# RWKV units of a hybrid diffusion step: half-height chunk factors, chain products in one tile shape, triangular inversion from 16-blocks through DRAM

## Chip, cores, metric

The kernel runs on one core of a Trainium2 chip. The metric is the device time of one execution in microseconds (us); the figure quoted is the median of the runs of one kernel. Engines: PE (TensorE products; PEld is its weight load), DVE (VectorE), ACT (ScalarE), POOL (GpSimd), SP (SyncE, which here only issues DMAs).

## What is computed

Two groups of tokens, 512 latent ones and 128 context ones, pass two layers of SwiGLU, token mixing and SwiGLU. The change lies in the mixing of layer 0, whose RWKV-7 half is, per head and direction, a scan over the tokens:

```python
def step(S, inp):
    r_t, w_t, k_t, v_t, kk_t, a_t = inp
    sa = jnp.einsum('bhvk,bhk->bhv', S, -kk_t)
    S = (S * w_t[:, :, None, :] + sa[..., None] * (kk_t * a_t)[:, :, None, :]
         + v_t[..., None] * k_t[:, :, None, :])
    return S, jnp.einsum('bhvk,bhk->bhv', S, r_t)
...
for d, (wd, ad) in enumerate(((wd_f, ad_f), (wd_b, ad_b))):
    ...
    yd, sd = wkv_scan(r32, decay, kd, v32, kk, a, s0[:, d], reverse=(d == 1))
```

There are 8 heads of 64 and two directions. The other half of the mixing is attention (8 query heads, 128 queries at a time); both end in one output projection. All of it is float32.

## The kernel before

The order of instructions on the engines' queues comes from a scheduler that works on a simulated timeline; the program's own order ranks what is ready. Loads are kept in order behind one another (`load`, L73).

Layer 0's mixing has a stage of its own, `rwkv_attention` (from L669), that runs from about 728 to 1366 us of the trace. Its work is cut into 4 units of two heads, each unit in both directions and in 10 chunks of 64 tokens. Each unit has four parts, all generators, and `take` lets them take turns:

- `rwkv_prep` loads r, k and v of the unit (one buffer each for r and k, so the loads for the next unit wait for this one's last reader), makes the decays, the scaled factors and, per chunk, one 128 x 256 product `pA` (L1020). Its stationary side `bk` holds b and k of both heads on 128 partitions; its moving side `arb` holds a and r of each head with zeros in the other head's rows. So L1000 to L1003 work on 64 partitions at a time, and L1004 copies the half that counts into `ar`. The product, masked (L1024), is `am`. The transposes of `bk` are `bt` (L1030, L1032).
- `tri_inverse` turns the strictly triangular 64 x 64 part of each of the unit's 40 chunk matrices (10 chunks, 2 directions, 2 heads) into the inverse of I - A. DVE block transposes bring the two 32 x 32 diagonal blocks to one chunk per partition (L1180), 30 steps of a multiply and an add on growing and shrinking blocks solve them (L1189, L1191), more transposes bring them back (L1199, L1202), and two rounds of 40 products of 32 x 32 make the block off the diagonal (L1210, L1218).
- `rwkv_chain` has 10 jobs, 8 latent and 2 context chunks, each for two heads and two directions. One after the other: `am` by values and `ar` by state into PSUM (L1086, L1097), a copy to `rt` (L1099), the inverse times `rt` (L1102), a copy to `uv` (L1104), the next state from the identity times the old state plus `bt` times `uv` (L1090, L1110), scaled by the decay (L1113), and the read-out in PSUM `ps_yr` from `uv` and from the state (L1121, L1123), added to `yb` (L1128).
- `rwkv_out` normalises, gates and stores `yc` (L1158).

Attention (`att_block`, 40 blocks) is put between them by `take`; its results go out by SP (L893). The context's final states go out by SP too (L1138), and their tile shares its one buffer with the next unit's initial states. PSUM tiles of tag `ps` have 3 buffers while the stage runs, `pn` 2 and `pb` 1; a tag's buffers are given out in program order. The order of the parts is:

```python
take(28, 5, prep(0))
take(16, 4, inv(0), prep(1))
take(12, 8, chain(0), inv(1))
take(10, 7, chain(1), prep(2), out(0))
take(12, 9, out(1), inv(2), prep(3))
take(12, 5, inv(3), chain(2))
take(12, 2, out(2), chain(3))
take(4, 0, out(3))
```

A product in float32 shows in the trace as two pairs of a weight load and a matmul; "x8" is four products.

Of the kernel before, what the change touches and what calls it, by code (L numbers as in the profile page):

```python
# [9 lines left out]
F32 = mybir.dt.float32  # L10
# [21 lines left out]
class K:  # L32
    """The network on one core. Activations are feature-major: [features, tokens]."""
# [29 lines left out]
    def open_res(self):  # L63
        """temporaries, weights raw and in two parts, input of the next product, residual."""
# [6 lines left out]
    def load(self, dst, src):  # L71
        """a load that the scheduler keeps behind the load before it."""
# [28 lines left out]
    def setup(self):  # L101
        """parameters and tokens; the loads that the first sub-layer waits for come first."""
# [11 lines left out]
            # these wait until the first sub-layer runs  # L114
# [7 lines left out]
        def rows_of(name):  # L122
            """rows of parameters ..."""
# [11 lines left out]
        def columns(name, rows):  # L135
            """... turned into one scalar per partition."""
# [26 lines left out]
        # silu of both condition vectors; 32 stationary columns, of which 2 are in use  # L163
# [15 lines left out]
        # tokens, feature-major  # L179
# [18 lines left out]
                # 1 + the bias of scale; gain of the output times the weight of the residual  # L198
# [40 lines left out]
    def ada(self, l, j, parts):  # L239
        """pieces of work that make mods[l, j][:, part, d, group]: shift, scale, gate of sub-layer j of layer l."""  # L240
# [13 lines left out]
    def ada_piece(self, l, j, part, t, w=None):  # L254
        """two of the eight input tiles; four groups of 256 outputs go to as many column groups of the array."""
# [24 lines left out]
        if part:  # L280
            # gain * (1 + scale), or weight * gate * gain
# [383 lines left out]
    def rwkv_attention(self):  # L665
# [5 lines left out]
        for h in range(2):  # L671
            self.nc.gpsimd.memset(self.arb[64 - 64 * h:128 - 64 * h, :, h], 0.0)
# [496 lines left out]
    def tri_inverse(self, u):  # L1169
# [15 lines left out]
        for s in range(1, 31):  # L1185
# [6 lines left out]
            if s % 6 == 0:  # L1192
                yield
# [705 lines left out]
```

## Time and profile before

| what | us |
|---|---|
| median of 3 runs (3339.91 to 3350.36) | 3347.76 |
| span of the profiled execution, first to last instruction | 3337.1 |
| PE busy in it | 3091.3 |
| DVE busy | 1923.3 |
| ACT busy | 1210.2 |
| POOL busy | 683.2 |

The profiled execution has no time of its own beside its span; the median of the runs stands 10.7 us above it, which is 0.3%. The chain of work that ended last is 80% PE and 10% DVE. Over most of the span PE is 90% busy or more; the slices from 728 to 1366 us, the stage of the change, are where it is not, and where the granted TensorE clock is lowest. Inside that stage the engines take turns at being the bound, so it is read in seven parts, by the parts of `take`.

### The profile page before, as it was taken

What the parts mean: (1) busy time and instruction counts of PE and PEld (TensorE: products, weight loads), DVE (VectorE), ACT (ScalarE), POOL (GpSimd) and SP (SyncE); (2) the same over time, 40 slices, a digit from 0 to 9 for tenths busy, and PEclk for the clock granted to TensorE, in tenths of its full rate; (3) what the DMA queues carried; (4) which work ended last, traced back from release to release, by engine and by line L of the source; (5) the groups of instructions that cost most, each with busy time, mean ns of one, the idle gap of its engine ahead of it and who ended that gap; (6) DMA issues with size and microseconds to landing.
All of it is one profiled execution on the core that took longest, in us unless ns stands there. A gap on an engine that the chain in (4) does not pass through costs nothing.

```text
span 3337.1 us, 55197 instructions
## 1 busy us (share of the span) xinstructions
PE 3091.3 (93%) x22259; PEld 2857.2 (86%) x22259; DVE 1923.3 (58%) x3731; ACT 1210.2 (36%) x2491; POOL 683.2 (20%) x795
## 2 busy tenths in 40 slices
PE   7999999986789789899999999999997689999998
PEld 6999998974576567789999999999996579999998
DVE  5433357428735861475466686666487955733346
ACT  4422235325334432453332453233353235422223
POOL 1000014132001200153333231233142533100002
PEclk8999999987778796899999999999998789999998
DMA  6433245620000000735443445454358863342223
GB/s 223 153 101 127 99 136 183 220 84 17 5 21 15 13 7 3 199 109 159 142 153 122 155 137 167 138 165 142 115 139 204 272 204 120 108 139 76 76 89 108
DMA packets 333924, 404.44 MB, mean 121 GB/s; under 512 B 42217, under 2 KB 299174, under 8 KB 333414
## 3 DMA queue, kind: packets, MB, share of 16 engines
q1 hardware_dynamic: 319174, 361.96, 34.4%
q0 software_dynamic: 14496, 38.97, 3.9%
q8 instruction: 175, 2.87, 0.4%
q14 instruction: 79, 0.65, 0.1%
HBM read 356.79 MB, written 42.89 MB: 120 GB/s over the span
## 4 chain that ended last, share of the span: by engine, by line
PE 80%; DVE 10%; issue 3%; POOL 2%; DMA 2%; ACT 2%; SPq 0%; POOLq 0%; DVEq 0%; ACTq 0%
PE ps_h L428 9%; PE ps_h L429 9%; PE ps_h L430 9%; PE ps_wide L428 5%; PE ps_wide L429 5%; PE ps_wide L430 5%; PE ps_y L428 5%; PE ps_y L430 5%; PE ps_y L429 5%; PE ps_wide L263 2%; PE ps_yr L1123 1%; PE ps_A L1020 1%; PE ps_pt L929 1%; PE ps_yr L1121 1%; DVE s5x L1564 1%
## 5 line engine op out<-in xcount | busy, mean ns | idle before, releaser
L401 DVE TENSOR_TENSOR wlo<-w,whi 128x1024 fp32r<-128x1024 f32 (+2 forms) x574 | 572.6, 1005 | 384.2 <-ACT whi L400 374.4
L400 ACT CAST whi<-w 128x1024 fp32r<-128x1024 f32 (+2 forms) x576 | 483.0, 847 | 857.0 <-PE ps_h L429 288.0
L428 PE MATMUL ps_h<-hh,whi 128*128 128x320 f32 x2112 | 658.0, 312 | 3.7 <-ACT hh L345 2.4
L429 PE MATMUL ps_h<-hl,whi 128*128 128x320 f32 x2112 | 656.7, 311 | 0.3 <-DVE hl L346 0.3
L430 PE MATMUL ps_h<-hh,wlo 128*128 128x320 f32 x2112 | 656.3, 311 | 0.0
L428 PEld LDWEIGHTS ps_h<-hh,whi 128*128 128x128 f32 x2112 | 399.2, 189 | 9.9 <-issue 3.4
L429 PEld LDWEIGHTS ps_h<-hl,whi 128*128 128x128 f32 x2112 | 398.8, 189 | 2.6 <-issue 1.5
L430 PEld LDWEIGHTS ps_h<-hh,wlo 128*128 128x128 f32 x2112 | 398.8, 189 | 1.1 <-issue 0.8
L429 PE MATMUL ps_y<-gl,whi 128*128 128x320 f32 x1056 | 325.8, 310 | 0.0
L430 PE MATMUL ps_y<-gh,wlo 128*128 128x320 f32 x1056 | 325.3, 310 | 0.0
L428 PE MATMUL ps_y<-gh,whi 128*128 128x320 f32 x1056 | 323.8, 311 | 1.1 <-ACT y L519 1.0
L428 PE MATMUL ps_wide<-hh,whi 128*128 128x320 f32 x912 | 288.6, 316 | 10.6 <-ACT y L653 4.4
L429 PE MATMUL ps_wide<-hl,whi 128*128 128x320 f32 x912 | 286.4, 314 | 1.3 <-DVE hl L346 1.2
L430 PE MATMUL ps_wide<-hh,wlo 128*128 128x320 f32 x912 | 285.3, 313 | 0.0
L362 POOL TENSOR_TENSOR ssy<-ssy,sq 128x320 f32<-128x320 f32 x84 | 96.0, 1142 | 566.1 <-ACT sq L361 563.5
L428 PEld LDWEIGHTS ps_y<-gh,whi 128*128 128x128 f32 x1056 | 197.1, 188 | 6.5 <-ACT y L519 2.2
L430 PEld LDWEIGHTS ps_y<-gh,wlo 128*128 128x128 f32 x1056 | 197.9, 188 | 1.0 <-issue 0.8
L429 PEld LDWEIGHTS ps_y<-gl,whi 128*128 128x128 f32 x1056 | 198.2, 188 | 0.7 <-issue 0.5
L428 PEld LDWEIGHTS ps_wide<-hh,whi 128*128 128x128 f32 x912 | 174.2, 191 | 17.9 <-issue 5.3
L470 DVE SCALAR_TENSOR_TENSOR g<-th,ps_h 128x320 f32<-128x320 f32 x159 | 77.0, 485 | 175.9 <-PE ps_h L430 175.3
L429 PEld LDWEIGHTS ps_wide<-hl,whi 128*128 128x128 f32 x912 | 173.7, 190 | 3.3 <-DVE hl L346 1.9
L430 PEld LDWEIGHTS ps_wide<-hh,wlo 128*128 128x128 f32 x912 | 173.6, 190 | 0.6 <-DVE wlo L401 0.3
(461 smaller groups left out, 5916.8 us busy)
## 6 DMA issues: line engine op xcount, KB each, us to landing
w<-in_ffn_w_dram SPq DMA_DIRECT2D x120, 1024.0 KB
ada_w<-in_ada_w_dram SPq DMA_DIRECT2D x72, 1024.0 KB
w<-in_ffn_w_dram SPq DMA_DIRECT2D x112, 512.0 KB
w<-in_ab_w_in_dram SPq DMA_DIRECT2D x14, 1024.0 KB
s5cd<-s_work POOLq DMA_DIRECT2D x128, 64.0 KB, 2.4
s5bd<-s_st POOLq DMA_DIRECT2D x32, 256.0 KB, 3.1
s5bt<-s5bd SPq DMA_DIRECT2D x32, 256.0 KB
w<-in_s_w_out_dram SPq DMA_DIRECT2D x8, 1024.0 KB
```

The costliest lines, as they stand in the source:

```text
L263: nc.tensor.matmul(ps[32 * g:32 * g + 32, :256], self.sc[:, 2 * t + k, :], w[:, k, g * 256:g * 256 + 256], start=(t + k == 0), stop=(2 * t ...
L362: nc.gpsimd.tensor_tensor(ss, ss, sq, op=OP.add)
L400: a = self.nc.scalar.copy(hi[:, :kt], s)
L401: v = (eng or self.nc.vector).tensor_tensor(lo[:, :kt], s, hi[:, :kt].bitcast(F32), op=OP.subtract)
L428: nc.tensor.matmul(o, hi[:, k], ah[k][half], start=(k == 0), stop=False)
L429: nc.tensor.matmul(o, hi[:, k], al[k][half], start=False, stop=False)
L430: self.last[0] = nc.tensor.matmul(o, lo[:, k], ah[k][half], start=False, stop=(k == kt - 1))
L470: nc.vector.scalar_tensor_tensor(g, t, 0.5, p3[:, :HALF], op0=OP.mult, op1=OP.mult)
L929: nc.tensor.matmul(po, self.vt[:, b, rows], pts[:, n], start=(n == 0), stop=(n == nkt - 1))
L1020: nc.tensor.matmul(pA[:, j % 2 * 256:j % 2 * 256 + 256], bk[:, j].rearrange("p a t -> p (a t)"), arb[:, j].rearrange("p h a t -> p (h a t) ...
L1121: nc.tensor.matmul(py[hr, col(d)], uv[:, d, p, h], rv(am[:, d, p, h, 64:]), start=True, stop=first)
L1123: nc.tensor.matmul(py[hr, col(d)], s[hr, d, p], rv(u["ar"][d][hr, self.chunk(d, p), 1]), start=False, stop=True)
```

## The change

It touches the four units alone (and removes comments elsewhere). The diff, cut to its core:

```diff
 rwkv_attention:
-        self.arb = self.mixe.tile([128, 10, 2, 2, 64], F32, name="arb")
+        self.st = [self.mixb.tile([128, 2, 2, 64], F32, name=f"st{k}") for k in range(4)]
+        for t in self.st:
+            for h in range(2):
+                mset(t[64 - 64 * h:128 - 64 * h, :, h], 0.0)
+        self.dx = [self.mixe.tile([128, 20, 64], F32, name=f"inv_d{k}") for k in range(2)]
+        self.invd = [self.dram.tile([2, 80, 256], F32, name=f"invd{k}") for k in range(2)]
+        self.invx = [self.dram.tile([2, 2, 80, 256], F32, name=f"invx{k}") for k in range(2)]
 rwkv_prep:
-            for h in range(2):
-                ...
-                nc.scalar.copy(ar[hr], arb[hr, :, h])
+            nc.vector.scalar_tensor_tensor(ar[:, :, 0, 1:], kc[:, :, 1:], -2.0, e2[:, :, :63],
+                                           op0=OP.mult, op1=OP.mult)
+            nc.vector.tensor_scalar(ar[:, :, 0, :1], kc[:, :, :1], -2.0, None, op0=OP.mult)
+            nc.gpsimd.tensor_tensor(ar[:, :, 1], rc, e2, op=OP.mult)
...
+            for j0, j1 in ((0, 2), (2, 6), (6, 10)):
+                pA = [self.ps("ps_A") for _ in range(2)]
+                for j in range(j0, j1):
+                    for h in range(2):
+                        hr = slice(64 * h, 64 * h + 64)
+                        nc.tensor.matmul(pA[h][:, (j - j0) * 128:(j - j0 + 1) * 128],
+                                         bk[hr, j].rearrange("p a t -> p (a t)"),
+                                         ar[hr, j].rearrange("p a t -> p (a t)"), start=True, stop=True)
 rwkv_chain (dr[d] is rows 64 d to 64 d + 63; the values of direction d lie on dr[1 - d]):
+            for h in range(2):
+                for d in range(2):
+                    nc.tensor.matmul(b[dr[d], col(h)], am[:, d, p, h, :64], uv[:, d, p, h],
+                                     start=(h == 0), stop=(first and h == 1))
+            if not first:
+                for d in range(2):
+                    nc.tensor.matmul(b[dr[d], :128], u["ar"][d][:, self.chunk(d, p), 0],
+                                     s[:, d].rearrange("p h c -> p (h c)"), start=False, stop=True)
+            nc.scalar.copy(rt[:64, 0], b[:64, :128])
+            nc.vector.tensor_copy(rt[64:, 1], b[64:, :128])
+            if not first and p != 7:
+                for d in range(2):
+                    for h in range(2):
+                        nc.tensor.matmul(b2[dr[h], col(d)], self.ident[:, dr[h]], s[:, d, h],
+                                         start=(d == 0), stop=False)
...
+                for h in range(2):
+                    dst = fin[dr[h]] if new is None else new[dr[h], :, h]
+                    nc.vector.tensor_tensor(dst, b2[dr[h], :128].rearrange("p (d c) -> p d c", c=64),
+                                            ec[dr[h], :, p][:, :, None].to_broadcast([64, 2, 64]), op=OP.mult)
...
+                    nc.tensor.matmul(py[dr[h], col(d)], uv[:, d, p, h], rv(d, am[:, d, p, h, 64:]),
+                                     start=(d == 0), stop=(first and d == 1))
...
+                        nc.tensor.matmul(py[dr[h], col(d)], s[:, d, h],
+                                         rv(d, u["ar"][d][:, self.chunk(d, p), 1]), start=False, stop=(d == 1))
 tri_inverse (all new; at[d] is the A part of am for direction d):
+        for d in range(2):
+            for b in range(4):
+                nc.sync.dma_start(
+                    invd[d, 20 * b:20 * b + 20].rearrange("i (s t) -> s i t", t=16),
+                    at[d][16 * b:16 * b + 16, :, 16 * b:16 * b + 16])
+        mset(self.dx[0].rearrange("p i t -> p (i t)"), 0.0)
+        nc.sync.dma_start(xa.rearrange("q d s t -> q d (s t)"), invd.rearrange("d q e -> q d e"))
+        for d in range(2):
+            nc.gpsimd.tensor_tensor(at[d], at[d], self.offm[dr[d], None, :].to_broadcast([64, 20, 64]), op=OP.mult)
+        for s in range(1, 15):
+            ...   # per direction a multiply and an add on [80, n * s], n = 15 - s
+        nc.sync.dma_start(invx.rearrange("w d q e -> q (w d) e"), xx.rearrange("q w d t s -> q (w d) (t s)"))
+        for w in range(2):
+            for d in range(2):
+                for b in range(4):
+                    r = slice(64 * d + 16 * b, 64 * d + 16 * b + 16)
+                    nc.sync.dma_start(self.dx[w][r, :, 16 * b:16 * b + 16],
+                                      invx[w, d, 20 * b:20 * b + 20].rearrange("i (r c) -> r i c", c=16))
+        groups = ((0, 8), (8, 16), (16, 20))
+        two = lambda: [self.ps("ps_n") for _ in range(2)]
+        ...   # nn = at dd; then three times y = e + nn y, groups of chunks, d = 0 and 1 in turn:
+                        nc.tensor.matmul(ps[d][dr[d], (i - i0) * 64:(i - i0 + 1) * 64], nn[dr[d], i], y[dr[d], i],
+                                         start=True, stop=True)
+                for d in range(2):
+                    nc.vector.tensor_tensor(out, e[dr[d], i0:i1], ps[d][dr[d], :n].rearrange(
+                        "p (i t) -> p i t", t=64), op=OP.add)
```

So the 16 x 16 diagonal blocks of all chunks of a unit are inverted on 80 partitions; the rest of the inverse is a product series that ends after three rounds, because the matrix of 4 x 4 blocks off the diagonal is nilpotent. The products of `nn`, and each of the three rounds, are 40 products of 64 x 64 x 64 per unit.

## Rows read from the trace of the kernel before

**Rows 1.** Windows, the stage: us, PE, PEld, DVE, ACT, POOL busy; clock, DMA.

```profile
728.00:790.00 62.00, 46.41 (x169) 30.89 (x168) 35.08 (x53) 29.21 (x52) 23.22 (x18) 0.67 0.07 23
790.00:877.00 87.00, 56.02 (x359) 41.24 (x358) 72.84 (x124) 35.22 (x66) 14.31 (x9) 0.73 0.06 19
877.00:980.00 103.00, 91.61 (x783) 70.52 (x781) 55.58 (x133) 30.77 (x81) 2.38 (x2) 0.78 0.01 3
980.00:1078.00 98.00, 91.02 (x691) 68.31 (x689) 44.77 (x96) 43.82 (x103) 17.16 (x9) 0.88 0.09 28
1078.00:1174.00 96.00, 72.60 (x452) 52.37 (x451) 75.63 (x143) 45.42 (x92) 18.80 (x11) 0.82 0.04 12
1174.00:1270.00 96.00, 85.37 (x807) 67.16 (x804) 55.35 (x135) 31.27 (x84) 1.56 (x2) 0.86 0.02 8
1270.00:1347.00 77.00, 73.79 (x530) 56.52 (x530) 13.82 (x46) 12.00 (x40) 2.79 (x2) 0.65 0.02 5
```

**Rows 2.** Windows, tile ps_c (chain products): us, PE, PEld, DVE, ACT busy; clock, DMA.

```profile
877.00:980.00 103.00, 35.28 (x320) 26.85 (x320) 8.23 (x29) 5.16 (x20) 0.78 0.01 3
980.00:1078.00 98.00, 26.63 (x320) 20.87 (x320) 7.95 (x29) 5.15 (x20) 0.88 0.09 28
1174.00:1270.00 96.00, 32.93 (x320) 24.97 (x320) 8.25 (x29) 5.17 (x20) 0.86 0.02 8
1270.00:1347.00 77.00, 39.49 (x320) 30.52 (x320) 8.27 (x29) 5.18 (x20) 0.65 0.02 5
1331.50:1339.10 7.60, 4.48 (x34) 3.46 (x34) 0.86 (x3) 0.52 (x2) 0.50 0.01 2
```

**Rows 3.** Windows, tile ps_yr (read-out): us, PE, PEld, DVE busy; clock, DMA.

```profile
877.00:980.00 103.00, 24.14 (x152) 17.41 (x152) 2.88 (x10) 0.78 0.01 3
980.00:1078.00 98.00, 20.12 (x136) 14.49 (x136) 2.58 (x9) 0.88 0.09 28
1174.00:1270.00 96.00, 21.50 (x152) 15.59 (x152) 2.87 (x10) 0.86 0.02 8
1270.00:1347.00 77.00, 26.98 (x152) 19.49 (x152) 2.69 (x10) 0.65 0.02 5
```

**Rows 4.** Timeline of PE in one late chain job: start, length, line, tiles, shape, count.

```profile
1334.01 1.11 PE L1102 MATMUL ps_c<-rt,am 128*64 128x64 f32 x8 [0.39 <-ACT rt L1099]
...
1336.28 0.37 PE L1086 MATMUL ps_c<-uv,am 128*64 128x64 f32 x1
...
1336.78 0.42 PE L1121 MATMUL ps_yr<-am,uv 128*64 128x64 f32 x2
...
1339.15 0.69 PE L1086 MATMUL ps_c<-uv,am 128*64 128x64 f32 x4
```

**Rows 5.** Windows, tile t11v, then tile ps_A: us, PE, PEld, DVE (then ACT) busy.

```profile
728.00:1366.00 638.00, 28.89 (x640) 26.81 (x640) 15.15 (x8) 6.00 (x12) 0.78 0.06 19
728.00:1366.00 638.00, 56.95 (x160) 36.98 (x160) 27.46 (x40) 0.78 0.06 19
```

**Rows 6.** Windows, tile inv_x, the whole stage: us, DVE, ACT, POOL busy; clock, DMA.

```profile
728.00:1366.00 638.00, 129.59 (x264) 4.18 (x4) 0.63 (x4) 0.78 0.06 19
```

**Rows 7.** Groups by line on DVE, 728 to 1366: busy us, mean ns, idle before.

```profile
L1180 DVE STREAM_TRANSPOSE inv_a<-am 32x1024 f32<-32x1024 f32 x16 | 30.8, 1925 | 8.7 <-PE ps_z L1218 8.4
...
L1024 DVE TENSOR_TENSOR am<-ps_A,k_amask 128x512 f32<-128x512 f32 x40 | 27.5, 689 | 23.5 <-PE ps_A L1020 23.3
...
L1000 DVE SCALAR_TENSOR_TENSOR arb<-kkh,e 64x630 f32<-64x630 f32 x16 | 21.9, 1368 | 0.3
...
L1191 DVE TENSOR_TENSOR inv_x<-inv_x,inv_t 128x30 f32<-128x30 f32 x8 | 1.6, 200 | 0.2
```

**Rows 8.** DMA, 2480 to 2500 us (stores in 160-byte pieces): packets, MB, share of 16 engines.

```profile
q1 hardware_dynamic: 7401, 1.20, 59.5%
```

**Rows 9.** The page's DMA issues: count, KB each, median us to landing.

```profile
s5cd<-s_work POOLq DMA_DIRECT2D x128, 64.0 KB, 2.4
```

**Rows 10.** Waits of SP's queue, 728 to 1366: total us, times, longest us.

```profile
SPq L893 <- ACT att_out L930: 375.8, 20, 42.9
```

More of the change, by code (lines that the diff above doesn't have):

```diff
@@ L1058, in rwkv_chain, with new_state @@
                                         self.ident)
[L1059 to L1064 removed]
+                nc.scalar.copy(uv[dr[1 - d], d, p:p + n].rearrange("p j h c -> p (j h c)"), pv[:64, :n * 128])
+        def new_state():
+            self.st.append(self.st.pop(0))
+            return self.st[-1]
         sin = self.mixb.tile([64, 2, 2, 64], F32, name="s_in", tag="s_io", bufs=1)
@@ L1112, in rwkv_chain @@
-                dst = fin if p == 9 else s[:, :, p + 1]
-                nc.vector.tensor_tensor(dst, b2[:, :128].rearrange("p (d c) -> p d c", c=64),
-                                        ec[:, :, p][:, :, None].to_broadcast([128, 2, 64]), op=OP.mult)
+                for d in range(2):
+                    for h in range(2):
+                        nc.tensor.matmul(b2[dr[h], col(d)], u["bt"][d][:, self.chunk(d, p), dr[h]], uv[:, d, p, h],
+                                         start=(first and d == 0), stop=(d == 1))
@@ L1125, in rwkv_chain @@
+            if not first:
+                for d in range(2):
+                    for h in range(2):
+                        nc.tensor.matmul(py[dr[h], col(d)], s[:, d, h],
+                                         rv(d, u["ar"][d][:, self.chunk(d, p), 1]), start=False, stop=(d == 1))
             c0, c1 = self.chunk(0, p), 9 - self.chunk(1, p)
@@ new lines, in tri_inverse @@
+        yield
+        dd, e = self.dx
+        groups = ((0, 8), (8, 16), (16, 20))
+        f2 = lambda ap: ap.rearrange("p i t -> p (i t)")
+        two = lambda: [self.ps("ps_n") for _ in range(2)]
+        nn = self.mixe.tile([128, 20, 64], F32, name="inv_n", bufs=1)
+        for i0, i1 in groups:
+            ps = two()
+            for i in range(i0, i1):
+                for d in range(2):
+                    nc.tensor.matmul(ps[d][dr[d], (i - i0) * 64:(i - i0 + 1) * 64], at[d][:, i], dd[dr[d], i],
+                                     start=True, stop=True)
+            for d, copy in ((0, nc.scalar.copy), (1, nc.vector.tensor_copy)):
+                copy(f2(nn[dr[d], i0:i1]), ps[d][dr[d], :(i1 - i0) * 64])
+            yield
@@ new lines, in tri_inverse @@
+        y = e
+        for step in range(3):
+            for i0, i1 in groups:
+                ps = two()
+                n = (i1 - i0) * 64
+                for i in range(i0, i1):
+                    for d in range(2):
+                        nc.tensor.matmul(ps[d][dr[d], (i - i0) * 64:(i - i0 + 1) * 64], nn[dr[d], i], y[dr[d], i],
+                                         start=True, stop=True)
+                for d in range(2):
+                    out = (dd[dr[d], i0:i1], at[d][:, i0:i1])[step == 2]
+                    nc.vector.tensor_tensor(out, e[dr[d], i0:i1], ps[d][dr[d], :n].rearrange(
+                        "p (i t) -> p i t", t=64), op=OP.add)
+                yield
+            y = dd
```

179 lines of the change are left out of this document (65 added, 114 removed).

## Prediction

> **What bounds the kernel now.** I read the windows of the RWKV stage first [rows 1]. The reader should see that the bound changes from part to part. I call the seven rows A to G. In C, D, F and G, where a chain runs, PE is busy 91.6 of 103, 91.0 of 98, 85.4 of 96 and 73.8 of 77 us. In B and E, where an inversion runs beside a preparation, DVE leads instead, with 72.8 of 87 and 75.6 of 96. The clock column matters too: 0.65 in G, where little but a chain runs, against 0.88 in D.
>
> Next come the windows cut to the chain's own products [rows 2] and its read-out [rows 3]. They make up 59.4 us of PE in C, 46.8 in D, 54.4 in F and 66.5 in G, for ten jobs each. Within one late job the clock is 0.50, the lower of the two levels (1.2 GHz) [rows 2].
>
> The timeline of that job shows how the time is spent [rows 4]. Four products that all go to the same column half (L1102) take 1.11 us, 0.28 each. From 1336.28 to 1336.78 four products that go to the two column halves in turn take 0.50, 0.125 each: they run side by side. From 1336.78 to 1339.15 six read-out products, which switch between 128-row and 64-row tiles each time, take 2.37, 0.395 each. So the same small product costs 0.125, 0.28 or 0.395 by its neighbours, and the order of shapes is the price.
>
> Last I read the inversion: 28.9 us of PE over the four units [rows 5], and on DVE 129.6 us [rows 6] plus 30.8 us for the transposes in [rows 7], together 160.4, or 40.1 a unit.
>
> **The change, part by part.** The sum is made against the profiled execution, whose span is 3337.1; the median stands 10.7 above it, and I carry the difference over to the median of 3347.8.
>
> Chain. A full job now has 26 products, all in one shape (128 rows, 64 columns) and issued to the two column halves in turn: 26 x 0.125 = 3.25, and 0.25 more because the two state products are twice as wide, so 3.5. The first context job has 16 products (2.0) and the last latent job 18 (2.5). A unit is 8 x 3.5 + 2.0 + 2.5 = 32.5 us of PE. That saves 26.9 in C, 14.3 in D, 21.9 in F and 34.0 in G. The bounds of a product are 0.125 and 0.28; I take 0.125 because that row has the same shapes and the same alternation. The new state takes two DVE products of about 0.28 in place of one (8.27 us for 29 instructions in G [rows 2]): 2.5 us more a unit, beside PE except in G.
>
> Inversion on PE. 160 products of 64 x 64 a unit, in turn on two tiles that share neither rows nor columns: 160 x 0.125 = 20.0 against 28.9 / 4 = 7.2 [rows 5], so 12.8 more a unit; at 0.28 each it would be 37.6 more.
>
> Inversion on DVE. 14 steps of 4 small operations at 0.20 [rows 7] are 11.2. The evictions are 3 rounds of two directions with 1280 columns each; 512 columns took 0.689 [rows 7], so 1.72 each and 10.3 in all, and DVE's share of the first product adds 1.7. That is 23.2 against 40.1, so 16.9 less a unit.
>
> Factors. L1000 works on all 128 partitions at once: 8 instructions for 16 of 1.368 us [rows 7], 2.7 less a unit; its POOL and ACT companions shrink likewise, off the bound. The chunk products `pA` become two of half the height and half the width. The old ones had 36.98 us of weight loads in 160 [rows 5], 0.231 each. Of the 320 new loads, none overlapping is 18.5 a unit and all overlapping in twos is 9.2, against 14.2 now (56.95 / 4). I take no gain, and 5 either way a unit as the bound.
>
> POOL. The mask of `am` (two operations of 64 x 1280 a unit) and the clearing of `dx` lie beside the DMAs and the 14 steps. POOL is busy 1.6 to 23 us in these parts [rows 1], so I cost them at nothing. If the cover goes, `nn` waits for the mask.
>
> DMAs. The inversion gets three trips through DRAM: 8 stores and a load, a store, and 16 loads. They come in 64-byte pieces, 2560 out and 5120 back. The nearest row is 160-byte pieces: 7401 packets in 59.5% of 16 engines over 20 us are 25.7 ns of one engine each [rows 8], so 4.1 and 8.2 us over 16 engines. A small DMA lands 2.4 us after its issue [rows 9]. The path of one inversion is then about 6.5 out, 2.9 in, 15 for the steps, 2.4 out, 10.6 in, and 28 for products and evictions: some 65 us. It runs beside a preparation or a chain, which cover it as long as the part is longer.
>
> By part, with the PE rows of [rows 1] scaled by the share that PE reaches:
> - A: L1000 alone, 3 less.
> - B: DVE falls to 72.8 - 19.6 = 53.2 and PE rises to 68.8, which leads. At the 89% that PE reaches in C this is 77, 10 less.
> - C: PE 91.6 - 26.9 + 12.8 = 77.5, by 103 / 91.6 gives 87, 16 less.
> - D: 91.0 - 14.3 = 76.7, by 98 / 91.0 gives 83, 15 less.
> - E: DVE 56.0, PE 72.6 + 12.8 = 85.4, at 89% it is 96: nothing. PE takes over from DVE.
> - F: 85.4 - 21.9 + 12.8 = 76.3, by 96 / 85.4 gives 86, 10 less.
> - G: PE 39.8. The wait from job to job is late next: three groups of products, two copies (0.26) and the two state products. I estimate 4.8 a job, 48 against 77, 29 less.
>
> The sum is 83 us less: 3347.8 - 83 = **3265**.
>
> **A rule against it.** Switching between tile shapes costs: 0.395 against 0.125 [rows 4]. The Trainium skill, TensorEngine Tiling (Array Packing), section Key Properties, says that changing the tiling mode, and not just the tile, drains the engine; the trace agrees. By that rule the change removes drains within the chain but brings a third shape, the inversion's 64 x 64, next to it. This is the second rival.
>
> **The rivals.**
> 1. *A queue takes the gain (slower).* The inversion's DMAs go through SP's queue in order, and there the stores of attention results wait: 375.8 us in 20 waits, 18.8 on average, the longest 42.9 [rows 10]. If each of the three trips stands behind one such wait, an inversion takes 65 + 56 = 121. B, C, E and F, which I put at 77, 87, 96 and 86, grow to 121, by 138 in all: 83 less becomes 55 more, **3403**. It decides for slower from about 42 us per inversion, where the four parts give back 83. For it: SP has just one queue, and any store that is late holds what follows. Against: the scheduler orders the queue by when things should be ready, and SP is idle for most of the stage. Chance 0.09.
> 2. *The shapes mix.* If half of the products of the chain (242 a unit) and the inversion (160) in C and F meet another shape before them, they cost 0.395 in place of 0.125: 54 us a part, 61 when scaled, 122 in both, so 39 more, **3387**. For it: the queue before mixes shapes freely in [rows 4]. Against: products of a job wait for the same copy and so stay together. Chance 0.05.
> 3. *It doesn't do what it says.* If the halves don't overlap, a product costs 0.28: a unit's chain takes 68 in place of 47 to 67, and the inversion 45 in place of 7. C and F alone lose about 50 each, and the whole comes to about 150 more, **3500**. Against: the 0.50 us of [rows 4]. Chance 0.03.
> 4. *Part of it is given back to PSUM.* The new parts take two of the three buffers of `ps` at a time, so a second pair waits for an eviction. 12 groups a unit at 0.9 us, none hidden, give back 43: **3308**, and with further waits up to no change. For it: chain, attention and inversion share the same three buffers. Chance 0.13, of which 0.04 no change.
> 5. *More.* If the parts are set by their dependences rather than by PE, C and F fall to the inversion's 70, D to 68, E to 75, B to 70 and G to 42: 165 less, **3183**. For it: PE's busy time holds modelled ends and drains that go with the switches. Chance 0.15.
>
> **How the numbers follow.** My forecast has 0.55 and its own range is 3223 to 3303, half the gain more or less. About 0.3% (10 us) is what a measurement of this kernel can tell from no change. Faster by more: 0.55 + 0.15 + 0.09 = 0.79, and I give 0.80; within it 0.04; slower 0.16, which is rivals 1 to 3. The range that leaves out no more than 2 in 10 reaches from the fifth rival to no change: 3185 to 3345.
>
> **What would show it.** In the new profile the chain's products in the part with the last chain should take 33 us of PE, in two column halves in turn, with no switch in a job. DVE should spend some 23 us a unit on the inversion. E should stay near 96 with PE leading, and G should fall below 50. Wrong would be: an idle PE before the inversion's products, waiting for a DMA that SP issued late (rival 1); products at 0.395 in C and F (rival 2); or PE waiting on evictions of `ps` (rival 4).

## The result, and the profile after

The changed kernel takes **3271.4 us** (median of 4 runs, 3267.9 to 3278.6) beside 3348.0 for the kernel before on the same chip: ratio 0.977, 95% interval 0.976 to 0.979. The forecast was 3265, the range 3185 to 3345. The profiled execution after has a span of 3271.2 us, against 3337.1 before: 65.9 less.

The copies that take a unit's final states out of PSUM mark the end of each chain, in every kernel here. After (line, engine, count, min/median/max ns, first and last start):

```profile
L1154 ACT COPY s_out<-ps_fin x2: 362/362/363, 966.2 to 1051.6; 64x256 f32<-64x256 f32 x2
L1154 ACT COPY s_out<-ps_fin x2: 367/368/369, 1233.5 to 1278.2; 64x256 f32<-64x256 f32 x2
```

Before (the same columns):

```profile
L1136 ACT COPY s_out<-ps_fin x2: 360/363/366, 982.2 to 1085.5; 64x256 f32<-64x256 f32 x2
L1136 ACT COPY s_out<-ps_fin x2: 366/366/366, 1266.5 to 1347.2; 64x256 f32<-64x256 f32 x2
```

So, in us, A to C became 16.0 shorter, D 17.9 (103.3 to 85.4), E and F together 0.9 longer (181.0 to 181.9), and G 36.0 shorter (80.7 to 44.7): 69.0 in all. The forecast had 29, 15, 10 and 29. The places are not those of the forecast: D and G gave more, the parts with an inversion much less.

The windows of the stage, cut at the turns of the new kernel (us, then PE, PEld, DVE, ACT, POOL busy, clock, DMA share and GB/s; they answer to [rows 1]):

```profile
731.00:806.00 75.00, 57.13 (x235) 40.48 (x235) 35.32 (x57) 29.34 (x58) 23.76 (x22) 0.66 0.14 41
806.00:886.00 80.00, 72.77 (x533) 59.77 (x532) 47.00 (x124) 24.70 (x53) 18.13 (x10) 0.66 0.11 19
886.00:971.00 85.00, 74.31 (x964) 59.36 (x962) 42.31 (x152) 33.20 (x83) 5.95 (x5) 0.88 0.09 16
971.00:1055.00 84.00, 75.45 (x774) 59.50 (x773) 46.16 (x108) 39.54 (x98) 18.91 (x11) 0.88 0.11 34
1055.00:1160.50 105.50, 92.62 (x636) 74.25 (x635) 58.47 (x149) 40.60 (x89) 20.08 (x11) 0.74 0.11 23
1160.50:1236.50 76.00, 66.55 (x944) 55.43 (x943) 38.62 (x144) 27.39 (x74) 5.37 (x4) 0.91 0.10 16
1236.50:1279.00 42.50, 33.75 (x538) 26.59 (x537) 16.47 (x55) 11.97 (x37) 1.98 (x1) 0.92 0.04 13
```

PE leads in all seven now; in B and E it has taken over from DVE, as forecast. But in E it is busy for 92.6 of 105.5 us, where the forecast had 85.4 of 96. And the clock in G is 0.92, where before it was 0.65.

The chain in C, D, F and G, first its own products, then the read-out (columns as above, without the engines that have no part; they answer to [rows 2, 3]):

```profile
886.00:971.00 85.00, 21.70 (x332) 16.25 (x332) 10.91 (x38) 5.16 (x20) 0.88 0.09 16
971.00:1055.00 84.00, 22.50 (x332) 17.43 (x332) 10.83 (x38) 5.12 (x20) 0.88 0.11 34
1160.50:1236.50 76.00, 19.47 (x332) 14.66 (x332) 10.88 (x38) 5.18 (x20) 0.91 0.10 16
1236.50:1279.00 42.50, 20.83 (x332) 15.40 (x332) 10.82 (x38) 5.17 (x20) 0.92 0.04 13
...
886.00:971.00 85.00, 8.21 (x152) 6.56 (x152) 2.88 (x10) 0.88 0.09 16
971.00:1055.00 84.00, 8.68 (x152) 7.41 (x152) 2.88 (x10) 0.88 0.11 34
1160.50:1236.50 76.00, 7.85 (x152) 6.29 (x152) 2.87 (x10) 0.91 0.10 16
1236.50:1279.00 42.50, 8.26 (x152) 6.49 (x152) 2.79 (x10) 0.92 0.04 13
```

In G that is 20.8 + 8.3 = 29.1 us of PE (66.5 before), in F 27.3 and in D 31.2. A record is half a product here: 332 + 152 records for 242 products. A late job on PE's timeline (start, length, line, records; it answers to [rows 4]):

```profile
1267.18 0.45 PE L1116 MATMUL ps_c<-rt,am 128*64 128x64 f32 x8 [0.51 <-DVE rt L1107]
1267.99 0.34 PE L1123 MATMUL ps_c<-uv,bt 128*64 128x64 f32 x4 [0.36 <-ACT uv L1119]
...
1268.60 0.40 PE L1141 MATMUL ps_yr<-ar,st 128*64 128x64 f32 x8
1268.84 0.40 PE L1098 MATMUL ps_c<-uv,am 128*64 128x64 f32 x8
...
1270.53 0.45 PE L1116 MATMUL ps_c<-rt,am 128*64 128x64 f32 x8 [0.51 <-DVE rt L1107]
```

From one L1116 to the next are 3.35 us; four products (L1141) take 0.24 us until the next group starts, 0.06 each. What a job waits for now are the copies to `rt` and `uv`.

The groups of the new parts over 700 to 1300 (busy us, mean ns of one, idle before; L1261 and L1249 are the inversion's products, L1028 is `pA`, and the DVE lines are the inversion's evictions and steps; they answer to [rows 5 to 7]):

```profile
L1261 PE MATMUL ps_n<-inv_d,inv_n 64*64 64x64 f32 x960 | 67.5, 246 | 0.9 <-DVE inv_d L1265 0.6 <-DVE am L1032 0.2
L1028 PE MATMUL ps_A<-ar,bk 64*128 64x128 f32 x320 | 47.7, 351 | 13.4 <-DVE bk L1014 13.2
L1249 PE MATMUL ps_n<-inv_d,am 64*64 64x64 f32 x320 | 31.0, 282 | 7.0 <-DMA inv_d<-invx 7.0
L1265 DVE TENSOR_TENSOR inv_d<-inv_d,ps_n 64x512 f32<-64x512 f32 (+1 forms) x48 | 28.6, 596 | 18.1 <-PE ps_n L1261 17.1
...
L1222 DVE TENSOR_TENSOR inv_t<-inv_a,inv_x 80x14 f32<-80x14 f32 (+6 forms) x112 | 18.1, 193 | 5.1 <-ACT inv_x L1215 4.7
L1226 DVE TENSOR_TENSOR inv_x<-inv_x,inv_t 80x14 f32<-80x14 f32 (+6 forms) x112 | 17.8, 193 | 0.2
L1265 DVE TENSOR_TENSOR am<-inv_d,ps_n 64x512 f32<-64x512 f32 (+1 forms) x24 | 14.3, 597 | 9.7 <-PE ps_n L1261 9.1
```

The inversion's products take 98.5 us of PE, 24.6 a unit; DVE's lines 78.8 with 7.3 more for its copies, 21.5 a unit. The waits of SP's queue, 720 to 1300 (total us, times, longest; to [rows 10]):

```profile
SPq L902 <- ACT att_out L939: 217.8, 18, 41.3
SPq L1200 <- DVE am L1032: 57.1, 7, 14.4
...
SPq L1231 <- ACT inv_x L1230: 36.1, 4, 12.9
```

At the head of the queue the inversion's stores still wait for what they carry (L1200, L1231), so the queue is not what holds them.

### The profile page after: what moved, and what is told of

Read it like the earlier page. It is cut to its first block, busy times and chain, and to the rows that moved or that the text cites. A ratio compares the mean times of both kernels' runs of the same rounds, so it can differ in the third digit from the quotient of the medians.

```text
span 3271.2 us, 57170 instructions
## 1 busy us (share of the span) xinstructions
PE 3046.6 (93%) x23107; PEld 2847.9 (87%) x23107; DVE 1853.9 (57%) x3787; ACT 1193.0 (36%) x2463; POOL 699.1 (21%) x812
## 4 chain that ended last, share of the span: by engine, by line
PE 58%; DVE 6%; DMA 3%; POOL 2%; ACT 2%; issue 2%; SPq 1%; POOLq 0%; DVEq 0%; ACTq 0%
PE ps_h L428 7%; PE ps_h L429 7%; PE ps_h L430 7%; PE ps_y L428 4%; PE ps_y L429 4%; PE ps_y L430 4%; PE ps_wide L428 4%; PE ps_wide L429 4%; PE ps_wide L430 4%; PE ps_n L1261 1%; DVE s5x L1612 1%; PE ps_wide L263 1%; PE ps_pt L938 1%; DMA s5ud<-s5us 1%; DVE sj L1609 1%
```

## The experiments

All times are medians of 4 runs or more (10 for the read-out in two shapes) beside runs of the kernel before on the same chip. Not all kernels were run together: the kernel before has medians of 3340.7 to 3348.0 beside them, so a difference of some 7 us between two rows can be this alone. In the chain ends, four numbers stand for the four units.

| kernel | us | ratio to before, 95% |
|---|---|---|
| the change | 3271.4 | 0.976 to 0.979 |
| before, new chain alone | 3252.6 | 0.971 to 0.974 |
| that, and unpadded factors | 3273.4 | 0.976 to 0.981 |
| that, factors in turn | 3232.0 | 0.965 to 0.968 |
| the change, chain sorted by half | 3277.3 | 0.979 to 0.982 |
| the change, read-out in two shapes | 3354.4 | 1.002 to 1.006 |
| the change, factor operations split | 3281.2 | 0.979 to 0.983 |
| the change, late mask | 3272.2 | 0.977 to 0.981 |
| the change, no trip back | 3234.3 | 0.966 to 0.970 |
| the change, inversion in turn | 3226.1 | 0.963 to 0.966 |
| the change, one tile per group | 3206.7 | 0.958 to 0.961 |
| that, and factors in turn | 3202.5 | 0.957 to 0.959 |
| that, and two queues back | 3197.8 | 0.955 to 0.959 |

**The chain alone.** The kernel before with only the chain's jobs rewritten:

```diff
-                    nc.tensor.matmul(b[:64, col(d)], am[:, d, p, h, :64], uv[:, d, p, h],
-                                     start=(d == 0), stop=(first and d == 1))
+                    nc.tensor.matmul(b[dr[d], col(h)], am[:, d, p, h, :64], uv[:, d, p, h],
+                                     start=(h == 0), stop=(first and h == 1))
...
-                        nc.tensor.matmul(py[hr, col(d)], s[hr, d, p], rv(u["ar"][d][hr, self.chunk(d, p), 1]),
-                                         start=False, stop=True)
+                        nc.tensor.matmul(py[dr[h], col(d)], s[:, d, h],
+                                         rv(d, u["ar"][d][:, self.chunk(d, p), 1]), start=False, stop=(d == 1))
...
```

> The kernel before with nothing but the new chain (one tile shape, states block-diagonal over both heads); the old preparation with padded factors and the old inversion stay. Theory 1 (the gain is the chain's: its products run side by side in one shape, and PE bounds C, D, F and G): the chain falls to some 30 us of PE a unit here too, C, D, F and G become shorter by 27, 14, 22 and 30 us and B and E stay at 87 and 96, so 3250 to 3275, at or below the whole change. Rival (the change needs the relief of DVE by the new inversion: with the old one DVE's 40.1 us a unit take over as the bound of C and F): only D and G become shorter, by 15 and 30, so 3295 to 3320.

Measured: 3252.6, so theory 1 by the total. The ends were 959.4, 1047.6, 1218.2 and 1262.1: the stretches up to them (A to C, D, E and F, G) are shorter by 22.8, 15.1, 10.4 and 36.8 than before, so C gave less than theory 1 had, E and F together 10 where it had 22 for F, and G more. The chain alone gains more than the whole change; the other two parts cost 19 us together. For this gain DVE's relief by the new inversion was not needed.

**The chain sorted by column half.**

```diff
-            for h in range(2):
-                for d in range(2):
+            for d in range(2):
+                for h in range(2):
                     nc.tensor.matmul(b[dr[d], col(h)], am[:, d, p, h, :64], uv[:, d, p, h],
...
```

> The changed kernel with the chain's products sorted by column half (two in a row to the lower, two to the upper) instead of in turn; the same products in the same shapes. Theory 1 (the alternation is what makes the products run side by side, 0.125 us against 0.28 in the kernel before): every second product of 242 a unit stands behind one of its own half, so a product averages 0.2, the chain's PE rises from 30 to some 45 us a unit, and the time to 3300 to 3330. Rival (one shape is enough, and what was paid before was the switches alone; the order within four products does not matter): the chain stays within 3 us of 30, and the time at 3263 to 3280.

Measured: 3277.3, and its interval meets that of the change. In G the chain takes 22.2 + 9.6 = 31.8 us of PE in place of 29.1. The rival holds: turns of two are nearly as good as turns of one. The timeline of this kernel shows records of one group beside those of the next (L1098 and L1141 both start at 1265.44), so a half that is done early takes work of the group behind.

**The read-out in two shapes.**

```diff
-            if not first:
-                for d in range(2):
-                    for h in range(2):
-                        nc.tensor.matmul(py[dr[h], col(d)], s[:, d, h],
-                                         rv(d, u["ar"][d][:, self.chunk(d, p), 1]), start=False, stop=(d == 1))
+                    if not first:
+                        nc.tensor.matmul(py[dr[h], col(d)], s[dr[h], d, h],
+                                         rv(d, u["ar"][d][dr[h], self.chunk(d, p), 1]), start=False, stop=(d == 1))
```

> The changed kernel with the state's part of the read-out in 64-row tiles again, in turn with the 128-row products (as before the change); all else as it is. Theory 1 (each switch of shape costs: 0.395 us a product against 0.125): 8 products of each of 9 jobs a unit cost 0.27 more, 19 us of PE a unit, 2.2 a job. The read-out is not what the next job waits for, so G (some 42 us, PE 34) grows by half of it and C, D and F by all of it: 3310 to 3345. Rival (a switch costs nothing by itself, and the old order was slow for its column halves): the read-out stays near 8 us a unit, 3263 to 3280.

Measured: 3354.4, 83 more than the change and 8 more than before, above even theory 1. PE's timeline of this kernel in its last chain:

```profile
1338.45 0.42 PE L1136 MATMUL ps_yr<-am,uv 128*64 128x64 f32 x2
1338.80 0.47 PE L1139 MATMUL ps_yr<-ar,st 64*64 64x64 f32 x2
1339.20 0.47 PE L1136 MATMUL ps_yr<-am,uv 128*64 128x64 f32 x2
1339.61 0.47 PE L1139 MATMUL ps_yr<-ar,st 64*64 64x64 f32 x2
1340.01 1.65 PE L830 MATMUL ps_hb<-ident,xb 128*128 128x128 f32 x6
```

One product (x2 records) after the other starts 0.39 us later on average: the 0.395 of [rows 4] again. And the clock went with it. The windows between the last two ends of chains, of this kernel and then of the change:

```profile
1298.40:1366.70 68.30, 62.10 (x555) 47.41 (x554) 16.65 (x56) 13.54 (x42) 1.97 (x1) 0.65 0.03 9
```

```profile
1233.50:1278.20 44.70, 35.61 (x556) 28.29 (x556) 17.04 (x57) 13.68 (x42) 2.00 (x2) 0.93 0.03 7
```

All but the same count of records, 62.1 us busy against 35.6, at a clock of 0.65 against 0.93: the shapes cost twice, by the switch and by the lower of the two levels (1.2 against 2.4 GHz), at which the part runs for most of its time. The Trainium skill, TensorEngine Tiling (Array Packing), Key Properties, says that a change of tiling mode drains the engine; the trace agrees, with 0.39 us a product here. Four products of one shape that share a column half took 0.28 each [rows 4], at the lower level too. So some 0.11 of the 0.39 is the switch, by estimate, and the rest of the difference to a product in turn is the overlap that is lost.

**The factors' operations split.**

```diff
-            nc.vector.scalar_tensor_tensor(ar[:, :, 0, 1:], kc[:, :, 1:], -2.0, e2[:, :, :63],
+            for h in range(2):
+                hr = slice(64 * h, 64 * h + 64)
+                nc.vector.scalar_tensor_tensor(ar[hr, :, 0, 1:], kc[hr, :, 1:], -2.0, e2[hr, :, :63],
...
```

> The changed kernel with the three operations that make the factors done in two halves of 64 partitions again: 16 DVE and 8 POOL instructions a stage more. Theory 1 (beside the new chain and inversion PE leads, DVE has room in C, D, F and G): DVE does 2.7 us a unit more, which shows only in A and B, 3268 to 3283. Rival (DVE, through what it shares with POOL, still sets A, B and E): A, B and E each grow by 5 or more, 3283 to 3300.

Measured: 3281.2, 10 more, at the upper end of theory 1's numbers and just under the rival's; its interval just meets that of the change. Joining the two halves is worth at most about what it was to save on DVE (2.7 a unit by the forecast). This run doesn't tell the two theories apart.

**The new chain and the unpadded factors, with the old inversion.** The run of the chain alone, with the change's L1008 to L1038 in place of `arb` and its 128-row products:

```diff
-                        nc.tensor.matmul(pA[:, j % 2 * 256:j % 2 * 256 + 256],
-                                         bk[:, j].rearrange("p a t -> p (a t)"),
-                                         arb[:, j].rearrange("p h a t -> p (h a t)"), start=True, stop=True)
+                        nc.tensor.matmul(pA[h][:, (j - j0) * 128:(j - j0 + 1) * 128],
+                                         bk[hr, j].rearrange("p a t -> p (a t)"),
+                                         ar[hr, j].rearrange("p a t -> p (a t)"), start=True, stop=True)
...
```

> The new chain and the new unpadded factors with the old inversion by 32-blocks: the whole change but for its inversion. The chain alone gave 3252.6 and the whole change 3271, so the other two parts cost 19 together. Theory 1 (the inversion costs it, by its products on PE and by its path through DRAM; the factors help, 10 us for the joined operations as the run with split ones says): 3235 to 3252. Rival (the unpadded factors cost it, with twice as many products of half the height and the longer A): 3262 to 3275, as with the whole change.

Measured: 3273.4, the rival's. The unpadded factors alone cost 21 (the four runs reach from 3261.0 to 3279.5), and the new inversion costs nothing on top of them. Most of it lies between the second and the third end (170.6 with padded factors, 188.7 with these). PE's busy time for `pA` is the same, 57.4 against 57.3. So the suspicion against the inversion alone fell, and the next runs asked what the two parts have in common.

**One tile per group of the inversion.**

```diff
-            ps = two()
+            ps = self.ps("ps_n")
...
-                        nc.tensor.matmul(ps[d][dr[d], (i - i0) * 64:(i - i0 + 1) * 64], nn[dr[d], i], y[dr[d], i],
+                        nc.tensor.matmul(ps[dr[d], (i - i0) * 64:(i - i0 + 1) * 64], nn[dr[d], i], y[dr[d], i],
...
+                if step < 2:
+                    nc.vector.tensor_tensor(dd[:, i0:i1], e[:, i0:i1], ps[:, :n].rearrange(
...
```

> The changed kernel with both directions of a group of the inversion in one PSUM tile: 12 tiles a unit from the ring of three in place of 24, and evictions over 128 partitions at once where both directions end in one place (per unit DVE has 6 additions of 128 rows for 12 of 64, 0.6 us each). Theory 1 (my fourth rival: the ring of three holds the inversion, whose products and evictions take 50 us a unit where 28 were forecast): that phase falls to 30 to 40 us, and the time by 15 to 50, to 3220 to 3256. Rival (the phase is long because PE is shared, with the low clock, and by the order of the work): DVE has 3.6 us a unit less and no more than that shows, 3257 to 3273.

Measured: 3206.7, 65 less, more than theory 1 had. But the trace showed another thing than the ring. PE's timeline of this kernel, and then of the change, both in the last inversion:

```profile
1142.07 0.68 PE L1247 MATMUL ps_n<-inv_d,am 64*64 64x64 f32 x16
...
1144.71 2.08 PE L1258 MATMUL ps_n<-inv_d,inv_n 64*64 64x64 f32 x64
```

```profile
1199.86 0.99 PE L1249 MATMUL ps_n<-inv_d,am 64*64 64x64 f32 x8
...
1205.08 1.15 PE L1261 MATMUL ps_n<-inv_d,inv_n 64*64 64x64 f32 x32
...
1206.43 1.14 PE L1261 MATMUL ps_n<-inv_d,inv_n 64*64 64x64 f32 x16
```

With one tile 64 records take 2.08 us, 0.065 a product. In the change one run of 32 takes 1.15 (0.072 a product) and the next, of only 16, takes 1.14 (0.14): the same products at half the pace, with a granted clock of 1.00 in all three. The order in PE's queue says why. In the change it begins so (line, tile written, products):

```
L1249 MATMUL ps_n_7786<-inv_d0_7237,am_7276 64x64 x8
L1249 MATMUL ps_n_7787<-inv_d0_7237,am_7276 64x64 x8
L1249 MATMUL ps_n_7809<-inv_d0_7237,am_7276 64x64 x8
L1249 MATMUL ps_n_7810<-inv_d0_7237,am_7276 64x64 x8
```

The code writes the directions in turn, but the scheduler has mostly put all products of one tile first. Of the inversion's 640 products 450 stand right behind one of their own tile, 129 behind one of the other direction's. The run of 32 at 1205.08 is one that was left in turn; the 16 at 1206.43 are eight products of one tile. Where eight of one direction stand right before eight of the other, the trace of the change has (clock 1.00 here too):

```profile
876.62 1.90 PE L1261 MATMUL ps_n<-inv_d,inv_n 64*64 64x64 f32 x32 [0.30 <-DVE inv_d L1265]
```

That is 1.90 us for as many records as took 1.15 in turn. Products of one direction use the same rows and columns of the array, and the trace shows them one after the other; those of two directions run side by side when they stand in turn. With one tile for both there is nothing to sort: 589 products of this kernel stand behind one of the other direction.

**The mask late.** POOL's masks of `am` moved behind the 14 steps:

```diff
-        for d in range(2):
-            nc.gpsimd.tensor_tensor(at[d], at[d], self.offm[dr[d], None, :].to_broadcast([64, 20, 64]), op=OP.mult)
...
             if s % 7 == 0:
                 yield
+        for d in range(2):
+            nc.gpsimd.tensor_tensor(at[d], at[d], self.offm[dr[d], None, :].to_broadcast([64, 20, 64]), op=OP.mult)
```

> The changed kernel with POOL's two masks of am (5.8 us a unit) put behind the 14 steps in place of before them; the same work. Theory 1 (the mask was not free: in A and B it holds POOL's factors of the next preparation and stretches DVE's, 3.5 us for 1.66): A or B become shorter by 3 to 10, 3255 to 3268. Rival (POOL has room and nothing waited): 3268 to 3278. If the mask then holds the inversion's first product, each unit loses up to 5.8, 3278 to 3295.

Measured: 3272.2, no difference. That POOL's mask costs nothing was right in the prediction.

**No trip back.** The store of `invx` and the 16 loads into `dx` are left out:

```diff
-        nc.sync.dma_start(invx.rearrange("w d q e -> q (w d) e"), xx.rearrange("q w d t s -> q (w d) (t s)"))
...
-                    nc.sync.dma_start(self.dx[w][r, :, 16 * b:16 * b + 16],
-                                      invx[w, d, 20 * b:20 * b + 20].rearrange("i (r c) -> r i c", c=16))
```

> The changed kernel without the way back through DRAM: the store of the inverted 16-blocks and the 16 loads that put them in block-diagonal form are left out, and the products run on what the tile holds, so the time is of a kernel without this transfer. Theory 1 (an inversion is a path of dependent steps that a part waits for: some 13 us of store, issue and landing a unit): B, C, E and F become shorter by up to 13 each, 3225 to 3255. Rival (the path is covered by the preparation or chain beside it, PE's sum sets the parts): 3260 to 3275.

Measured: 3234.3, 37 less: theory 1. The path of the inversion does set part of the stage. The stretches up to the ends became shorter by 15.6, 3.8, 10.4 and 0.8 us, mostly where an inversion runs. These are 30.6; the rest of the 37 lies behind the last of them, where no inversion runs.

**The inversion's products in turn.** Tiles and evictions of the change, the order enforced:

```diff
-                        nc.tensor.matmul(ps[d][dr[d], (i - i0) * 64:(i - i0 + 1) * 64], nn[dr[d], i], y[dr[d], i],
-                                         start=True, stop=True)
+                        self.turn(nc.tensor.matmul(ps[d][dr[d], (i - i0) * 64:(i - i0 + 1) * 64], nn[dr[d], i],
+                                                   y[dr[d], i], start=True, stop=True))
...
+    def turn(self, product):
+        i = product.ins
+        if self.last_turn:
+            self.tc.add_manual_dep(
+                i, self.last_turn, mybir.DependencyInfo(mybir.DependencyClass.NoSync, mybir.DependencyReason.DATA),
+                reason="products in turn")
+        self.last_turn = i.name
```

> The changed kernel with the inversion's products held in the order in which the code writes them, one direction and the other in turn (each product is told to follow the one before). Tiles, evictions and everything else are as in the change: 24 tiles a unit, two taken at a time. In the changed kernel's instruction order the eight products of one direction's tile come first and then the eight of the other, and its trace has 16 of them in 1.14 us where the run with one tile has 64 in 2.08. Theory 1 (the 65 us of that run came from the order: the two directions run side by side only when they alternate): ps_n falls from some 25 to some 14 us of PE a unit, and the time to 3205 to 3230. Rival (they came from the ring of three, two tiles at a time): ps_n may become cheaper but the products wait for evictions, and the time stays at 3255 to 3285, since a strict order only adds waits.

Measured: 3226.1, theory 1: 45 of the 65 us (by the ratios 42 of 60) come from the order alone, with two tiles at a time as before. Now 580 products stand behind one of the other direction and none behind one of its own. The groups of the inversion's products:

```profile
L1271 PE MATMUL ps_n<-inv_d,inv_n 64*64 64x64 f32 x960 | 46.1, 233 | 5.8 <-DVE am L1275 2.4 <-DVE inv_d L1275 2.4 <-DVE am L1040 0.7
...
L1258 PE MATMUL ps_n<-inv_d,am 64*64 64x64 f32 x320 | 20.0, 288 | 9.4 <-DMA inv_d<-invx 6.1 <-ACT att_p L931 2.8 <-ACT inv_n L1261 0.5
```

66.1 us in place of 98.5. PE waits 5.8 for evictions here (0.9 in the change): the ring of three is the next thing, and it or the smaller evictions make the 19 us that one tile per group gains over this. Those two were not tried apart.

**One tile per group, and the factors' products in turn.**

```diff
-                        nc.tensor.matmul(pA[h][:, (j - j0) * 128:(j - j0 + 1) * 128],
+                        self.turn(nc.tensor.matmul(pA[h][:, (j - j0) * 128:(j - j0 + 1) * 128],
...
```

> The run with one tile per group of the inversion, and besides it the products of the factors (ps_A) held in the code's order, one head's 64 rows and the other's in turn. In the instruction order of the change four of one head come first, then four of the other. The run with the old inversion put the cost of the unpadded factors at 21 us. Theory 1 (that cost is the same as the inversion's: halves that lie in different tiles are sorted by tile and no longer run side by side): ps_A falls from 47.7 us of PE to 25 to 32, and the time from 3206.7 to 3185 to 3198. Rival (the cost is twice as many products and evictions in pairs of tiles, whatever their order): ps_A stays above 42 and the time at 3200 to 3213.

Measured: 3202.5. `pA` did fall nearly as theory 1 has it, but the time moved by 4, within the rival's numbers and no more than the rows can tell apart:

```profile
L1037 PE MATMUL ps_A<-ar,bk 64*128 64x128 f32 x320 | 32.4, 319 | 15.0 <-DVE bk L1022 12.9 <-DVE inv_d L1270 1.6 <-DVE am L1274 0.4
```

So 11 us of PE (43.8 to 32.4) are worth little here. In the kernel with one tile per group the ends were 932.1, 1018.7, 1170.6 and 1214.8, here 925.6, 1013.0, 1168.3 and 1212.6: the first unit gains 6.5, and E and F give 3.4 back.

**Two queues for the way back.** In the kernel above, the half of `invx` that the first products need is stored before ACT's copies and loaded by SP's queue, the other half by POOL's:

```diff
-        nc.sync.dma_start(invx.rearrange("w d q e -> q (w d) e"), xx.rearrange("q w d t s -> q (w d) (t s)"))
+        for w, queue in ((0, nc.sync), (1, nc.gpsimd)):
...
+            queue.dma_start(invx[w].rearrange("d q e -> q d e"), xx[:, w].rearrange("q d t s -> q d (t s)"))
...
```

> The kernel of the run before in this list (one tile per group, both heads in turn), with the way back through DRAM split: the half that the first products need is stored before ACT's transposing copies and loaded by SP's queue, the other half goes by POOL's queue beside it. Theory 1 (the path of dependent steps still sets part of the stage, as the run without the way back said with 37 us for 13 us a unit): the first half lands some 5 us earlier a unit, and the time is 5 to 20 below that run's. Rival (with shorter products the path is covered by the work beside it, or POOL's issues hold its own work): within 5 us of that run or above it.

Measured: 3197.8, 5 less; the intervals of the two overlap, so rival and theory stay open. It is the fastest kernel here: 0.957 of the kernel before, and 74 us below the change.

**The old inversion, and the factors in turn.** The same edit of `pA` in the kernel with the old inversion:

```diff
-                        nc.tensor.matmul(pA[h][:, (j - j0) * 128:(j - j0 + 1) * 128],
+                        self.turn(nc.tensor.matmul(pA[h][:, (j - j0) * 128:(j - j0 + 1) * 128],
...
```

> The new chain and the unpadded factors with the old inversion, and the factors' products (ps_A) held in the code's order, one head's 64 rows and the other's in turn. The same kernel with those products sorted by tile took 3273.4, with padded factors 3252.6. Theory 1 (the unpadded factors cost these 21 because their two halves ran one after the other, the more so in E at the lower clock): ps_A falls from 57.4 us of PE to 36 to 42 and the time to 3240 to 3258. Rival (order is worth 4, as in the run with one tile a group; the 21 lie in the waits for pairs of tiles or in POOL's longer operations): 3265 to 3275.

Measured: 3232.0, 41 less and below theory 1's numbers. The groups, without and with the order:

```profile
L1019 PE MATMUL ps_A<-ar,bk 64*128 64x128 f32 x320 | 57.4, 389 | 33.5 <-DVE bk L1005 28.6 <-DVE mx L916 4.7 <-DVE am L1023 0.2
```

```profile
L1028 PE MATMUL ps_A<-ar,bk 64*128 64x128 f32 x320 | 38.2, 357 | 22.4 <-DVE bk L1013 16.0 <-DVE mx L921 5.8 <-DVE am L1032 0.3
```

The 21 us that the unpadded factors cost are the order's, and 20 more that they gain over padded ones are set free by it. 19.2 us of PE gave 41 of time. Between the second and third end, where most of the cost lay, 188.7 became 170.0. DVE shows what hung on it. Its copies of `pA` to `am`, over 700 to 1366, without the order and with it (busy us, mean ns, idle before):

```profile
L1023 DVE TENSOR_TENSOR am<-ps_A,k_amask 128x512 f32<-128x512 f32 (+1 forms) x48 | 28.5, 600 | 45.2 <-PE ps_A L1019 44.9
```

```profile
L1032 DVE TENSOR_TENSOR am<-ps_A,k_amask 128x512 f32<-128x512 f32 (+1 forms) x48 | 27.1, 595 | 20.1 <-PE ps_A L1028 20.0
```

DVE waited 44.9 us for these products, 20.0 with the order; with padded factors it was 22.6. Beside one tile per group the same order shortens this wait only from 21.0 to 14.2. And there DVE is busy for 86 of the 152 us between the second and third end, here for 130 of 171. So a late product holds DVE most where DVE has the old inversion to do. That this makes the whole difference between 41 and 4 us is likely but not shown.

## Why the prediction was right, and where not

The sign was right for the reason given, the chain. That the total came within 7 us is luck: by the ends of the chains, D and G gave 54 us where 44 were forecast, and the parts with an inversion 15 where 39 were.

- **The chain** is the gain, as forecast. Its PE time was forecast at 32.5 us a unit and is 27.3 to 31.2 (the sums of the two windows' rows in F and D). By itself it gives 94 of time (3346.5 to 3252.6), where the change as a whole gives 77. At the lower level a product costs about 0.11: in the change, at a granted clock of 0.50 (1197.0 to 1199.9), groups of four start 0.43 apart from 1197.18 to 1198.03, where [rows 4] gave 0.125.
- **G**: forecast 48 for 4.8 a job, measured 44.7 and 3.35 a job. The step that was off is the price of a job, worked out at the lower level. That the clock would rise with one shape was not in the sum.
- **The inversion on DVE**: 21.5 a unit against 23.2 forecast. Right. But in the change it bought nothing that shows: with the old inversion in its place the time is 3273.4. It pays only when the products stand in turn: with the factors in turn the old inversion gives 3232.0, the new one with one tile per group 3202.5. How much of these some 29 us is DVE's relief was not tried apart.
- **The inversion on PE** is the first wrong step: "160 products of 64 x 64 a unit, in turn on two tiles that share neither rows nor columns: 160 x 0.125 = 20.0". They are not in turn in the queue. PE takes 24.6 a unit, partly at a higher clock; in turn it is 16.5, with one tile 14.2 (56.8 over the stage). E, where PE was forecast at 85.4 us, has 92.6 in its longer window.
- **The path of the inversion** is the second: "28 for products and evictions". From the first product (L1249) to the start of the last eviction (L1265) are 55, 55, 78 and 45 us in the four units: 828.7 to 884.0, 915.5 to 970.9, 1080.3 to 1158.5, 1188.2 to 1233.5. From the last stores of `am` on (805.9, 886.3, 1055.3, 1160.6) the path is 73 to 103 rather than 65. The order is part of it, but not all: with one tile per group products and evictions take 37 to 58 us, still more than 28. So the path is no longer covered by E or F: E + F, forecast at 10 less, came out 0.9 longer, and the run without the trip back shows that some 31 us of the stage hang on its way through DRAM.
- **The unpadded factors** were costed at "no gain, and 5 either way a unit". PE's busy time for `pA` is 47.7 against 56.95 before [rows 5], a gain of 2.3 a unit, within that; but the time rose by 21 in the run that has just this beside the chain. In that run PE is busy for `pA` as long as with padded factors (57.4 against 57.3), so the failed step is that the factors' price was looked for in PE's busy time alone. What rose is DVE's wait for `pA`, from 22.6 to 44.9, and with the two heads' products in turn it is 20.0 and the time 41 less.
- **A and L1000**: L1008 takes 13.3 us for 8, against 21.9 for 16 before: 2.1 a unit (2.7 forecast). A to C as a whole got 16 of the 29 forecast. Part of the rest is a late start: the first preparation's first activation is at 736.4 in the change and 729.7 before, its loads issue at 730.7 and 709.6. The run of the chain alone starts as late (735.9), so it is not the new inversion or the factors. What holds these loads was not tried.
- **The rivals.** The queue (1) and the shapes (2) did not come in; the run with the read-out in two shapes bears out the price put on the second (83 us for the 288 products in jobs that switch, 0.29 each, where it had 0.27). The halves overlap (3). The ring of `ps` (4) came near in its number but not in its mechanism: it had 43 given back by waits for evictions, and 65 is what one tile per group recovers. But 45 of them are the order of the products, which no rival had, and PE waits for evictions at L1261 for 0.9 us in the change; the ring's part is at most the 19 that are left. The dependences (5) would have given 3183, and the best kernel here stands at 3197.8.

## What to carry to other kernels

Products that are to run side by side in different parts of the array have to stand close in PE's queue: here turns of one or two did, turns of four and eight did not. This scheduler parted them when they wrote different PSUM tiles. Write both into one tile, or order them by dependences, and then look at the instruction order. When a change has three parts, time the strongest one alone: here it was worth more than the whole, and the difference named the fault.

## What was not expected of the hardware

- The clock followed the mix of shapes. In the part with the last chain it is 0.65 before [rows 1] and 0.65 with the read-out in two shapes, 0.93 in the change and 0.92 with the chain alone, though PE is busier by the record in the first two (73.8 of 77 us and 62.1 of 68.3, against 35.6 of 44.7).
- Turns of two on column halves are nearly as good as turns of one (3277.3 against 3271.4, with intervals that meet; 31.8 us of PE against 29.1 in G). Turns of eight on 64 x 64 tiles are far from it (32 records in 1.90 us, against 1.15 in turn).
- Two 64 x 64 products on different rows of the array run side by side although they write one PSUM tile, on different partitions (0.065 us a product with one tile per group, 0.072 with two tiles in turn).
